# First loads over two queues in another order, later sums of squares, and a later turn of the decay sums in a hybrid attention layer

## The chip, the core and the metric

The kernel runs on one core of a Trainium2 chip. The metric is device time in microseconds (us) for one execution. In the profile, PE is TensorE's matmul and PEld its weight load, ACT is ScalarE, DVE is VectorE, POOL is GpSimd, and SP is SyncE, which here only issues DMAs. A "q" behind an engine's name (ACTq) marks what its queue issues. Each engine works through its own queue in order.

## What is computed

One layer of a streaming encoder on x (512 frames by 1024 channels) and mem (256 memory tokens by 1024 channels), all in float32:

```python
u = rmsnorm(h, g_mix[l])
proj = u @ w_in[l]
(gq, gk, gv, gg, ga, fq, fk, fv, ff, mq, gates) = split_cols(proj, PROJ_SIZES)
...
log_a = jax.nn.log_sigmoid(ga @ w_alpha_up[l] + b_alpha[l]) / GLA_TAU
...
log_f = jax.nn.log_sigmoid(ff + b_forget[l])
o_fox = forgetting_attention(
...
mkv = rmsnorm(mem, g_mem[l]) @ w_mem_kv[l]
mk, mv = jnp.split(mkv, 2, axis=-1)
...
merged = gt[:, :, 0] * y_gla + gt[:, :, 1] * y_fox + gt[:, :, 2] * y_mem
h = h + merged @ w_out[l]
u2 = rmsnorm(h, g_ffn[l])
h = h + jnp.square(jax.nn.relu(u2 @ w_ff1[l])) @ w_ff2[l]
```

Branch A is a gated linear attention ("gla"), branch B the forgetting attention ("fox"), whose logits carry differences of F, the running sum of log_f over the frames; branch C attends to the memory tokens. Only the beginning matters here: the memory's keys and values, u, and the first projections.

## The kernel before

**Products.** Each float32 product is done with three matmuls on a high and a low part (`mm3`, L149 to L152: high x high, high x low, low x high). A weight block is 128 x 1024 float32, 512 KB. It is loaded (`raw`), ACT copies it to its rounded high part (`first_high`, or L141 for later blocks), and DVE subtracts to get the low part (`first_low`, L303, or L142). `gT` (L154) holds weights still and streams activations; `gN` (L164) does the reverse. Both are generators: one *unit* is the three matmuls for one block of 128 input channels, and the caller decides how many units PE gets before the next piece of work. PE's order is the order in which the program is written. PSUM has a pool of four banks with the tag "mm" and one of four with the tag "a".

**The first part** (L348 to L441) stands in `in_order`, which keeps ACT, DVE and PE in the written order. In this order:

- PE runs 12 warm-up matmuls on zeros (L327).
- ACT issues the DMA of `cols` (the gains, 16 KB). w0, the first weight block, is loaded in four quarters, three issued from ACT and the fourth from SP (`first_load(0, 4)`); mem comes from SP in four pairs of channel blocks (256 KB each) into `sg[0]` to `sg[2]` and `dct`. Then SP issues w1, w2, x's first pair, w3, x's other three pairs, the constants `cst`, and w4.
- For each of the 8 channel blocks of mem, ACT makes the high part times its gain (L370) and DVE the low part (L371), with the four quarters of w0 split in between; then w1, w2.
- Four key products of the memory, `mk_proj(0)` to `mk_proj(3)`, 24 matmuls of 256 columns each. Each holds one "mm" bank until `mk_take` (L342) copies it out on ACT. Between them stand the sums of squares of x (`x_squares`: square on ACT at L222 or L225, addition on DVE at L226) and the splits of w3 and w4.
- `rms_cols` (L231) adds up the squares over the partitions with PE; DVE and POOL (a power, L238) make 1/rms per frame. Then come the load and split of w5 and the loads of the rest.
- The memory's values, `mv`: 16 units of three matmuls with 512 columns, four for each of w4 to w7, into two "mm" banks. After six units, `bcast_rows` spreads 1/rms over the partitions (four scaled diagonals on ACT at L246, matmuls at L247, a copy to `rxb` at L249); w6 and w7 are split around it.
- `x_high` (L414 on DVE, L415 on ACT) and `x_low` (L418 on DVE) make u from x for each of 8 blocks; the splits of `both` (the block of the two low-rank projections; L426 on ACT, L428 on DVE), w9 and w10 (the first fox query and key weights) stand between them.

**The second part** (L650 on) runs the low-rank projection (L465, L466) interleaved with the first fox query and key, then fox's values `fv`, 32 units, with other work between them: after 4 units `decay_logs`, after 10 more `decay_sums` (running sums over frames on PE at L495 and L496, then a chain of small additions into `Fc` on DVE, L499 to L504), after 2 more `decay_rows` (PE turns `Fc` at L508, ACT negates it at L509 and issues seven small DMAs at L514). `mem_split` then squares mem on ACT and adds on DVE (L634 to L638), sums on PE (L231 again), and, in its second step, scales the memory's keys and values. `tc.issue_after(i)` makes what is written in its block wait in the queue behind instruction `i` on `i`'s engine, and on that engine alone.

ACT, DVE and POOL are ordered by the compiler's planner in the second part, PE by hand.

Of the kernel before, what the change touches and what calls it, by code (L numbers as in the profile page):

```python
# [61 lines left out]
def hybrid_block(ctx, tc, chunks, wst, xT, memT, xN, cols, gffn, gfin, wup, cst, out):  # L62
    nc = tc.nc
# [213 lines left out]
    with pool("front") as fp:  # L277
        rxb = sg[3]
        xr = fp.tile([P, KT, S], F32, name="xr")
        FIRST_W = [chunks[j] for j in range(8)] + [("G",), ("T", "w_in", OFF["fq"]), ("T", "w_in", OFF["fk"])]  # L280
        raws, ready, loads = {}, {}, {}

        def first_load(i, n=1):
            late = i in (3, 4, 7, 10)
            raws[i] = (fp if late else wp).tile([P, 1024], F32, tag="lead" if late else "raw", name=nm("raw"),
                                                bufs=2 if late else 3)
            for j in range(n):
                sl = slice(j * 1024 // n, (j + 1) * 1024 // n)
                loads[i] = (nc.scalar if n > 1 and j < 3 else nc.sync).dma_start(raws[i][:, sl], wst[index[FIRST_W[i]]][:, sl]).ins
                if n > 1:  # L290
                    yield

        def first_high(i, n=1, j=0):
            if i not in ready:
                ready[i] = [wp.tile([P, 1024], F32R, tag=g, name=nm(g)) for g in ("hi", "lo")]
            sl = slice(j * 1024 // n, (j + 1) * 1024 // n)
            cast = nc.scalar.copy(ready[i][0][:, sl], raws[i][:, sl])
            if i > 4:
                next_sum(cast.ins)

        def first_low(i, n=1, j=0):
            sl = slice(j * 1024 // n, (j + 1) * 1024 // n)
            nc.vector.tensor_tensor(ready[i][1][:, sl], raws[i][:, sl], f(ready[i][0][:, sl]), op=ALU.subtract)  # L303

        def first_split(i, n=1, j=0):
            first_high(i, n, j)
            first_low(i, n, j)

        def first_w(i):
            run(first_load(i))  # L310
            first_split(i)

        get_plain = get_w

        def get_first(key):
            return ready[FIRST_W.index(key)]

        get_w = get_first
        mxh = fp.tile([P, KT, M], F32R, name="mxh")
        mxl = fp.tile([P, KT, M], F32R, name="mxl")  # L320
        xacc = dct[:, :S]
        warm = fp.tile([P, 1], F32, name="warm")
        nc.vector.memset(warm, 0.0)
        wz = fp.tile([P, 512], BF16, name="wz")
        nc.gpsimd.memset(wz, 0.0)
        ps = at_()
        for _ in range(12):  # L327
            nc.tensor.matmul(ps, wz[:, :P], wz, start=True, stop=True)

        kv = {}  # L330

        def mem_in(k):
            return sg[k // 2][:, k % 2 * M:k % 2 * M + M] if k < 6 else dct[:, 4 * S + (k - 6) * M:4 * S + (k - 5) * M]

        def mk_raw(h):
            return gkT[h // 2][:, (h % 2) * M:(h % 2) * M + M]

        def mk_proj(h):
            return gT(("T", "w_mem_kv", P * h), mxh, mxl, lambda ps: kv.update({h: ps}), n=M)

        def mk_take(h):
            nc.scalar.copy(mk_raw(h), kv[h][:, :M])  # L342

        def x_squares(*ks):
            for k in ks:
                sq_col(fp, xr, S, k, xacc, "x")

        with in_order():  # L348
            nc.scalar.activation(warm, warm, AF.Exp)
            nc.scalar.dma_start(cols_s, cols)  # L350
            quarters = first_load(0, 4)
            for j in range(4):
                to = sg[j] if j < 3 else dct[:, 4 * S:5 * S]
                nc.sync.dma_start(to.rearrange("p (k t) -> p k t", k=2), memT[:, 2 * j:2 * j + 2])
                next(quarters)

            def x_load(j):
                nc.sync.dma_start(xr[:, 2 * j:2 * j + 2], xT[:, 2 * j:2 * j + 2])

            run(first_load(1), first_load(2))  # L360
            x_load(0)
            run(first_load(3))
            for j in range(1, 4):
                x_load(j)
            nc.sync.dma_start(cst_s[:, :2 * P], cst[:, :2 * P])
            nc.sync.dma_start(cst_s[:, 5 * P:], cst[:, 5 * P:])
            run(first_load(4))
            for k in range(KT):
                m = mem_in(k)
                nc.scalar.mul(mxh[:, k, :], m, gmem[:, k:k + 1])  # L370
                nc.vector.scalar_tensor_tensor(mxl[:, k, :], m, gmem[:, k:k + 1], f(mxh[:, k, :]),  # L371
                                               op0=ALU.mult, op1=ALU.subtract)
                if k % 2 == 0:
                    first_split(0, 4, k // 2)
            first_split(1, 2, 0)
            first_split(1, 2, 1)
            first_split(2)
            x_squares(0, 1)
            run(mk_proj(0))
            first_split(3)  # L380
            x_squares(2, 3)
            run(mk_proj(1))
            x_squares(4, 5, 6, 7)
            run(mk_proj(2))
            mk_take(0)
            mk_take(1)
            first_split(4)
            run(mk_proj(3))
            rx = rms_cols(fp, xacc, S)
            first_w(5)  # L390
            mk_take(2)
            mk_take(3)
            mv = gN([("N", "w_mem_kv", 2 * j, 512) for j in range(4)], of(mxh, mxl), 2, mmt,
                    lambda t, ps: kv.update({("v", t): ps}))
            for i in (6, 7):
                run(first_load(i))
            g_raw = load_w(("G",))
            for i in (9, 10):
                run(first_load(i))
            run(islice(mv, 6))  # L400
            put = bcast_rows(fp, rx, S, rxb)
            next(put)
            first_high(6)
            first_high(7)
            run(put)
            first_low(6)
            run(islice(mv, 6))
            with tc.issue_after(loads[7]):
                nc.sync.dma_start(cst_s[:, 2 * P:5 * P], cst[:, 2 * P:5 * P])
                nc.sync.dma_start(wup_s, wup)  # L410
            ends = {}

            def x_high(k):
                nc.vector.scalar_tensor_tensor(xr[:, k, :], xr[:, k, :], gmix[:, k:k + 1], rxb, op0=ALU.mult, op1=ALU.mult)  # L414
                ends[0] = nc.scalar.copy(uhi[:, k, :], xr[:, k, :]).ins  # L415

            def x_low(k):
                ends[1] = nc.vector.tensor_tensor(ulo[:, k, :], xr[:, k, :], f(uhi[:, k, :]), op=ALU.subtract).ins  # L418

            x_high(0)  # L420
            x_high(1)
            first_low(7)
            run(mv)
            x_low(0)
            raw3, w3 = (t.rearrange("p (k c) -> p k c", k=KT) for t in (g_raw, both))
            nc.scalar.copy(both, g_raw)  # L426
            low = slice(64, P)
            nc.vector.tensor_tensor(w3[:, :, low], raw3[:, :, low], f(w3[:, :, low]), op=ALU.subtract)  # L428
            first_high(9)
            x_high(2)  # L430
            x_low(1)
            first_low(9)
            x_high(3)
            x_low(2)
            first_split(10)
            for k in range(4, KT):
                x_high(k)
                x_low(k - 1)
            x_low(KT - 1)
            for t in range(2):  # L440
                nc.scalar.copy(gqT[t], kv["v", t])  # L441
        u_ends = ends[0], ends[1]
        get_w = get_plain
# [15 lines left out]
    with pool("fox") as xp:  # L459
# [32 lines left out]
        def decay_sums():  # L492
# [6 lines left out]
            nc.vector.tensor_copy(Fc[:, 0, :], cum[:, 0, :])  # L499
            nc.vector.tensor_copy(off[:, 0, :], tot[:, 0, :])  # L500
            for t in range(1, NT):
                nc.vector.tensor_tensor(Fc[:, t, :], cum[:, t, :], off[:, t - 1, :], op=ALU.add)
                if t < NT - 1:
                    nc.vector.tensor_tensor(off[:, t, :], tot[:, t, :], off[:, t - 1, :], op=ALU.add)  # L504

        def decay_rows():
            psT = at_()
# [121 lines left out]
        def mem_split():  # L629
            own = xp.tile([P, 4, M], F32, tag="nFb", name="memsum", bufs=4)  # L630
            acc, rmb = own[:, 0, :], own[:, 3, :]
            for k in range(KT):
                if k == 0:
                    nc.scalar.activation(acc, mem_in(0), AF.Square)  # L634
                else:
                    sq = own[:, 1 + k % 2, :]
                    nc.scalar.activation(sq, mem_in(k), AF.Square)
                    nc.vector.tensor_tensor(acc, acc, sq, op=ALU.add)  # L638
            rm = rms_cols(xp, acc, M)
            yield  # L640
            run(bcast_rows(xp, rm, M, rmb, 2))
# [11 lines left out]
        with tc.issue_after(u_ends[0]), tc.issue_after(u_ends[1]):  # L653
# [3 lines left out]
            z_end = decay_logs()  # L657
            run(islice(fv, 10))
            nc.vector.tensor_copy(msk_s, cst_s[:, 5 * P:5 * P + 64])
        decay_sums()  # L660
        run(islice(fv, 2))
        decay_rows()
        mem = mem_split()
        with tc.issue_after(z_end[0]), tc.issue_after(z_end[1]):
            next(mem)
        run(fv)
        run(fox_pair(1))
        run(mem)
# [922 lines left out]
```

## Time and profile before

| | |
|---|---|
| time, median of 3 runs | 808.89 us (808.88 to 809.57) |
| the profiled execution | 809.36 us |
| its span | 807.6 us |
| instructions | 12080 |
| busy DVE, ACT, POOL | 574.9, 458.3, 107.2 us |
| DMA traffic | 161.01 MB, mean 199 GB/s |

A row of a timeline has the start in us from the beginning of the span, the duration in us, the engine, the line, the operation, the tiles (written <- read), the shape and a count where several in a row are merged; in square brackets stands the idle time of the engine just before, and what ended it. A row of the waits says who waited for whom, for how long in total, how often, and the longest. A row of the windows has the stretch, its length, then for PE, PEld, DVE, ACT and POOL the busy time and the count of instructions, PE's granted clock, the DMA engines' share and GB/s. Instructions of one engine overlap a little: the next one starts some 0.1 us before the end of the one before.

### The profile page before, as it was taken

The page shows a single profiled execution, that of the slowest core. Times are in us where ns is not written, and L with a number is a line of the kernel's source. Part 1 is how long each engine was busy: PE and PEld are TensorE (multiplying, and loading weights), DVE is VectorE, ACT ScalarE, POOL GpSimd, SP SyncE. Part 2 cuts the span into 40 slices and gives each one's busy share as a digit, 9 for nine tenths or more (in the row PEclk, how much of TensorE's full clock was granted, in tenths as well). Part 3 has the DMA queues.
Part 4 walks back from the last instruction along what each step waited for, and adds up shares of the span by engine and source line. Part 5 has one row for each costly group of instructions (what it writes and reads, how often), then busy time and mean ns, then how long its engine had stood idle before and what let it go on. Part 6 is the DMA issues. An engine that isn't in the chain of part 4 may idle for free.

```text
span 807.6 us, 12080 instructions
## 1 busy us (share of the span) xinstructions
PE 795.8 (99%) x4617; PEld 679.5 (84%) x4617; DVE 574.9 (71%) x877; ACT 458.3 (57%) x727; POOL 107.2 (13%) x124
## 2 busy tenths in 40 slices
PE   9999999999999999999999999999999999999995
PEld 6887878778888888888888889988998899889984
DVE  6763756554565488496969658885788678878886
ACT  7575645533454446454645545764676477547764
POOL 0004221011001132111210000011001100100122
PEclk9999999999999999999999999999999999999998
DMA  9527779678668678889873706889668956895585
GB/s 338 210 92 228 236 228 241 202 209 215 203 209 225 194 218 172 177 212 235 213 179 106 285 3 222 228 197 212 218 176 190 249 196 166 196 258 185 152 153 147
DMA packets 41178, 161.01 MB, mean 199 GB/s; under 512 B 4968, under 2 KB 6048, under 8 KB 39072
## 3 DMA queue, kind: packets, MB, share of 16 engines
q0 software_dynamic: 11632, 60.56, 36.6%
q1 hardware_dynamic: 27504, 95.31, 33.8%
q10 hardware_dynamic: 1984, 4.37, 1.6%
q8 instruction: 36, 0.59, 0.3%
q14 instruction: 22, 0.18, 0.1%
HBM read 156.26 MB, written 31.49 MB: 232 GB/s over the span
## 4 chain that ended last, share of the span: by engine, by line
PE 93%; DVE 2%; DMA 1%; ACT 1%; issue 1%; SPq 0%; POOLq 0%; DVEq 0%; ACTq 0%
PE mm L150 20%; PE mm L151 19%; PE mm L152 19%; PE a L152 4%; PE a L150 4%; PE a L151 4%; PE mm L1020 3%; PE mm L1018 3%; PE mm L1019 3%; PE a L1018 2%; PE a L1020 2%; PE a L1019 2%; PE mm L1391 1%; PE a L616 1%; DMA raw<-in_wst_dram 1%
## 5 line engine op out<-in xcount | busy, mean ns | idle before, releaser
L201 ACT CAST hi<-raw 128x1024 fp32r<-128x1024 f32 x77 | 80.9, 1050 | 62.3 <-PE mm L151 34.3
L202 DVE TENSOR_TENSOR lo<-raw,hi 128x1024 fp32r<-128x1024 f32 x77 | 94.2, 1223 | 29.9 <-ACT hi L201 29.9
L142 DVE TENSOR_TENSOR wlo<-raw,whi 128x1024 fp32r<-128x1024 f32 x44 | 56.7, 1291 | 63.9 <-ACT whi L141 56.8
L141 ACT CAST whi<-raw 128x1024 fp32r<-128x1024 f32 x44 | 46.2, 1050 | 77.0 <-issue 27.5
L152 PE MATMUL mm<-u2h,lo 128*128 128x256 f32 x224 | 63.4, 283 | 0.0
L151 PE MATMUL mm<-u2l,hi 128*128 128x256 f32 x224 | 63.4, 283 | 0.0
L150 PE MATMUL mm<-u2h,hi 128*128 128x256 f32 x224 | 63.4, 283 | 0.0
L1303 POOL DMA_DIRECT2D Y<-in_wst_dram x32 | 27.4, 856 | 262.6 <-DVE lo L202 187.0
L201 ACT CAST hi<-Y 128x1024 fp32r<-128x1024 f32 x34 | 35.6, 1048 | 32.5 <-PE mm L152 22.0
L202 DVE TENSOR_TENSOR lo<-Y,hi 128x1024 fp32r<-128x1024 f32 x34 | 41.6, 1223 | 17.3 <-ACT hi L201 17.3
L150 PE MATMUL mm<-hi,ch 128*128 128x512 f32 x128 | 49.8, 389 | 0.0
L151 PE MATMUL mm<-lo,ch 128*128 128x512 f32 x128 | 49.8, 389 | 0.0
L152 PE MATMUL mm<-hi,cl 128*128 128x512 f32 x128 | 49.8, 389 | 0.0
L201 ACT CAST hi<-g 128x1024 fp32r<-128x1024 f32 x30 | 31.6, 1054 | 30.9 <-PE mm L1020 11.7
L202 DVE TENSOR_TENSOR lo<-g,hi 128x1024 fp32r<-128x1024 f32 x30 | 36.6, 1221 | 17.2 <-ACT hi L201 17.1
L150 PE MATMUL mm<-u2sh,hi 128*128 128x256 f32 x168 | 47.5, 283 | 0.0
L151 PE MATMUL mm<-u2sl,hi 128*128 128x256 f32 x168 | 47.5, 283 | 0.0
L152 PE MATMUL mm<-u2sh,lo 128*128 128x256 f32 x168 | 47.5, 283 | 0.0
L150 PE MATMUL mm<-uhi,whi 128*128 128x512 f32 x112 | 44.4, 397 | 0.0
L152 PE MATMUL mm<-uhi,wlo 128*128 128x512 f32 x112 | 43.7, 390 | 0.0
L151 PE MATMUL mm<-ulo,whi 128*128 128x512 f32 x112 | 43.6, 389 | 0.0
L151 PEld LDWEIGHTS mm<-u2l,hi 128*128 128x128 f32 x224 | 43.0, 192 | 0.2
(446 smaller groups left out, 2329.1 us busy)
## 6 DMA issues: line engine op xcount, KB each, us to landing
raw<-in_wst_dram SPq DMA_DIRECT2D x109, 512.0 KB, 4.9
Y<-in_wst_dram POOLq DMA_DIRECT2D x32, 512.0 KB, 5.4
raw<-T SPq DMA_DIRECT2D x28, 512.0 KB, 3.2
T<-in_wst_dram POOLq DMA_DIRECT2D x12, 1024.0 KB, 8.8
g<-in_wst_dram POOLq DMA_DIRECT2D x24, 512.0 KB, 5.9
Y<-in_wst_dram SPq DMA_DIRECT2D x16, 512.0 KB, 6.3
g<-in_wst_dram SPq DMA_DIRECT2D x12, 512.0 KB, 3.2
nFb<-dF ACTq DMA_DIRECT2D x8, 448.0 KB
```

The source lines that it names most:

```text
L141: cast = nc.scalar.copy(hi, raw)
L142: nc.vector.tensor_tensor(lo, raw, f(hi), op=ALU.subtract)
L150: nc.tensor.matmul(ps, lh, rh, start=start, stop=False)
L151: nc.tensor.matmul(ps, lh, rl, start=False, stop=False)
L152: nc.tensor.matmul(ps, ll, rh, start=False, stop=stop)
L201: nc.scalar.copy(hi, src)
L202: return nc.vector.tensor_tensor(lo, src, f(hi), op=ALU.subtract).ins
L616: nc.tensor.matmul(po[half[e], kt * P:], V[:, kt, 2 * j + e, :], PT[e][:, c0:c0 + S - kt * P], start=kt == 0, stop=kt == 3, skip_group_che ...
L1018: nc.tensor.matmul(ps[t], a, wh[:, kk, :], start=go, stop=False, **w)
L1019: nc.tensor.matmul(ps[t], a, wl[:, kk, :], start=False, stop=False, **w)
L1020: nc.tensor.matmul(ps[t], b, wh[:, kk, :], start=False, stop=k == 3, **w)
L1303: nc.gpsimd.dma_start(to, x, accum_op=ALU.add)
```

## The change

- Ten warm-up matmuls instead of 12.
- `cols` is issued from SP, ahead of mem; the first pair of mem goes in two halves; each quarter of w0 is issued before its pair of mem. w4 is loaded ahead of x's last pair and of the first constants, w5 before the values begin.
- w4 is split after six of x's eight squares instead of after all; three units of the values stand ahead of `rms_cols`, and w5 is split ahead of it. The broadcast follows after 8 units of the values instead of 6; w6 is split ahead of it, w7's low part and the cast of `both` directly behind it.
- `decay_rows` follows four units after `decay_sums` instead of two. The memory's squares are ordered behind the last addition of `decay_sums` (`f_end`) instead of the last of `decay_logs`, and the PE step over them (`rms_cols` in `mem_split`) comes 8 units later.

```diff
-        for _ in range(12):
+        for _ in range(10):
             nc.tensor.matmul(ps, wz[:, :P], wz, start=True, stop=True)
...
-            nc.scalar.dma_start(cols_s, cols)
+            nc.sync.dma_start(cols_s, cols)
             quarters = first_load(0, 4)
             for j in range(4):
                 to = sg[j] if j < 3 else dct[:, 4 * S:5 * S]
-                nc.sync.dma_start(to.rearrange("p (k t) -> p k t", k=2), memT[:, 2 * j:2 * j + 2])
+                to = to.rearrange("p (k t) -> p k t", k=2)
                 next(quarters)
+                if j == 0:
+                    for k in range(2):
+                        nc.sync.dma_start(to[:, k, :], memT[:, k])
+                else:
+                    nc.sync.dma_start(to, memT[:, 2 * j:2 * j + 2])
...
             run(first_load(1), first_load(2))
             x_load(0)
             run(first_load(3))
-            for j in range(1, 4):
-                x_load(j)
+            x_load(1)
+            x_load(2)
+            run(first_load(4))
+            x_load(3)
             nc.sync.dma_start(cst_s[:, :2 * P], cst[:, :2 * P])
             nc.sync.dma_start(cst_s[:, 5 * P:], cst[:, 5 * P:])
-            run(first_load(4))
...
             run(mk_proj(1))
-            x_squares(4, 5, 6, 7)
+            x_squares(4, 5)
+            first_split(4)
+            x_squares(6, 7)
             run(mk_proj(2))
             mk_take(0)
             mk_take(1)
-            first_split(4)
             run(mk_proj(3))
+            run(first_load(5))
+            mv = gN([("N", "w_mem_kv", 2 * j, 512) for j in range(4)], of(mxh, mxl), 2, mmt,
+                    lambda t, ps: kv.update({("v", t): ps}))
+            run(islice(mv, 3))
+            first_split(5)
             rx = rms_cols(fp, xacc, S)
-            first_w(5)
             mk_take(2)
             mk_take(3)
-            mv = gN([("N", "w_mem_kv", 2 * j, 512) for j in range(4)], of(mxh, mxl), 2, mmt,
-                    lambda t, ps: kv.update({("v", t): ps}))
             for i in (6, 7):
                 run(first_load(i))
...
-            run(islice(mv, 6))
+            run(islice(mv, 5))
+            first_split(6)
             put = bcast_rows(fp, rx, S, rxb)
             next(put)
-            first_high(6)
             first_high(7)
             run(put)
-            first_low(6)
+            first_low(7)
+            nc.scalar.copy(both, g_raw)
             run(islice(mv, 6))
...
             x_high(1)
-            first_low(7)
             run(mv)
             x_low(0)
             raw3, w3 = (t.rearrange("p (k c) -> p k c", k=KT) for t in (g_raw, both))
-            nc.scalar.copy(both, g_raw)
...
             for t in range(1, NT):
-                nc.vector.tensor_tensor(Fc[:, t, :], cum[:, t, :], off[:, t - 1, :], op=ALU.add)
+                end = nc.vector.tensor_tensor(Fc[:, t, :], cum[:, t, :], off[:, t - 1, :], op=ALU.add).ins
                 if t < NT - 1:
                     nc.vector.tensor_tensor(off[:, t, :], tot[:, t, :], off[:, t - 1, :], op=ALU.add)
+            return end
...
                     nc.vector.tensor_tensor(acc, acc, sq, op=ALU.add)
+            yield
             rm = rms_cols(xp, acc, M)
             yield
...
-        decay_sums()
-        run(islice(fv, 2))
+        f_end = decay_sums()
+        run(islice(fv, 4))
         decay_rows()
         mem = mem_split()
-        with tc.issue_after(z_end[0]), tc.issue_after(z_end[1]):
+        with tc.issue_after(z_end[0]), tc.issue_after(f_end):
             next(mem)
+        run(islice(fv, 8))
+        next(mem)
         run(fv)
         run(fox_pair(1))
         run(mem)
```

## The prediction

> **What bounds the kernel now.** I read the page first: engine totals, then the list of what PE waited for.
>
> ```profile
> PE 795.8 (99%) x4617; PEld 679.5 (84%) x4617; DVE 574.9 (71%) x877; ACT 458.3 (57%) x727; POOL 107.2 (13%) x124
> ...
> PE a L508 <- DVE Fc L502: 1.3, 1, 1.3
> PE a L328 <- POOL wz L325: 1.3, 1, 1.3
> PE a L231 <- DVE dct L226: 0.7, 1, 0.7
> ```
>
> PE is busy for 99% of the span, and that list of its waits is complete: three waits, all in the first 63 us. So no edit can win more than the late start of the real matmuls and the two waits at L231 and L508, and a wait that the edit creates in the front costs its full length. The change aims at exactly these three places. I take them in order of time, from the timelines of the single engines.
>
> ```profile
> 0.00:20.00 20.00, 18.51 (x108) 13.87 (x108) 12.82 (x24) 15.25 (x29) 0.73 (x5) 1.00 0.92 338
> 6.20:12.40 6.20, 6.20 (x37) 5.00 (x37) 5.87 (x14) 5.92 (x14) 0.00 (x0) 1.00 1.04 405
> ...
> 0.91 0.38 ACTq L350 DMA_DIRECT2D cols_s<-in_cols_dram  x1
> 1.32 5.03 PE L328 MATMUL a<-wz 128*128 128x512 bf16 x12 [1.32 <-POOL wz L325]
> 5.75 0.40 ACT L297 CAST hi<-raw 128x256 fp32r<-128x256 f32 x1 [0.78 <-DMA raw<-in_wst_dram]
> 6.20 0.39 PE L150 MATMUL mm<-mxh,hi 128*128 128x256 f32 x1
> ```
>
> In the windows the last two columns are the DMA share and GB/s: from 6.2 to 12.4 us all 16 DMA engines are full, at 405 GB/s, and the x loads further below, one each 1.3 us, show the same rate to 17.5. In that stretch a load can only come earlier if another comes later.
>
> **First loads and warm-up.** Two warm-up matmuls fewer save 2 x 0.42 us (5.03 us for 12); PE would be free at 5.5 instead of 6.35 us. The issue of cols (0.38 us) leaves ACT's queue, so the first quarter of w0 is issued 0.42 us earlier, and it no longer has cols ahead of it there; cols now stands on SP ahead of mem, at the same 0.4 us. SP issues one DMA more (mem pair 0 in two halves), some 0.4 us, while it has others in flight. The first real matmul waited for this quarter: the cast at 5.75 us ended DMA idle time and the matmul followed at 6.20. So real work begins 0.4 (issue alone) to 0.7 us (PE free) earlier; 0.6 taken. The last pair of mem now goes behind the fourth quarter, and everything after comes out of the full stream, so I let only 0.2 us of this reach the end of the four memory keys (0 to 0.6): PE gets there at 19.6 instead of 20.53 - 0.70 = 19.83. What stands next decides whether that counts.
>
> **x's squares and the turn of order at 20 us.**
>
> ```profile
> 16.14 1.16 ACT L225 ACTIVATE sq<-xr 128x512 f32<-128x512 f32 x2 [0.18 <-DMA xr<-in_xT_dram]
> 17.46 1.29 ACT L225 ACTIVATE sq<-xr 128x512 f32<-128x512 f32 x2 [0.16 <-DMA xr<-in_xT_dram]
> 18.66 0.63 ACT L342 COPY gkT<-mm 128x256 f32<-128x256 f32 x2
> 15.80 4.67 DVE L226 TENSOR_TENSOR dct<-dct,sq 128x512 f32<-128x512 f32 x6
> 20.39 1.22 DVE L303 TENSOR_TENSOR lo<-raw,hi 128x1024 fp32r<-128x1024 f32 x1
> 20.53 1.05 PE L231 MATMUL a<-cst_s,dct 128*128 128x1 f32 x8 [0.70 <-DVE dct L226]
> 21.44 0.48 PE L150 MATMUL mm<-hi,mxh 128*128 128x512 f32 x1
> ```
>
> Before, PE waits 0.70 us for the last sum of squares, runs L231 in 0.91 us, and begins the memory values at 21.44. Now three units of values (3 matmuls of 0.23 us each, 0.69 a unit) stand ahead of L231. They need three things. (a) w4 and its split: w4 is now loaded ahead of x's last pair, so it lands at about 17.46 and that pair one 512 KB place later, 17.46 + 1.32 = 18.78. (b) w4's low part: DVE does it after four of the six sums, 15.80 + 4 x 0.78 = 18.9, done 20.1; the last two sums end at 20.1 + 2 x 0.78 = 21.7 instead of 20.47. (c) a PSUM bank: the pool for these has four, the four key products fill them, and the first comes free with the first L342 copy, which in ACT's order stands behind the squares of x's last pair: 18.78 + 1.16 - 0.09 + 0.35 = 20.2. So (c) is last: the values begin at 20.2, whether PE was ready at 19.2 or 19.8. The 0.70 us wait is replaced by one of about 0.6. The three units end at 20.2 + 2.07 = 22.27, when the sums (21.7) are there, and L231 starts then: 1.74 us later than before, while PE's own work is 21.44 + 2.07 - (22.27 + 0.91) = 0.33 us ahead.
>
> **What hangs on L231.**
>
> ```profile
> 21.86 1.94 POOL L238 TENSOR_TENSOR rr<-ms,cst_s 128x4 f32<-128x4 f32 x1 [20.59 <-DVE ms L237]
> 23.83 1.28 ACT L246 ACTIVATE dg<-cst_s,rr 128x128 f32<-128x128 f32 x4 [1.67 <-POOL rr L238]
> 25.02 1.98 ACT L297 CAST hi<-raw 128x1024 fp32r<-128x1024 f32 x2
> 25.68 1.05 PE L247 MATMUL a<-dg,cst_s 128*128 128x128 f32 x8
> 26.49 0.48 PE L150 MATMUL mm<-hi,mxh 128*128 128x512 f32 x1
> 26.09 1.23 DVE L303 TENSOR_TENSOR lo<-raw,hi 128x1024 fp32r<-128x1024 f32 x1 [3.16 <-ACT hi L297]
> 27.52 1.42 DVE L414 SCALAR_TENSOR_TENSOR xr<-xr,cols_s,sg 128x512 f32<-128x512 f32 x2 [0.21 <-ACT sg L249]
> 28.85 1.22 DVE L303 TENSOR_TENSOR lo<-raw,hi 128x1024 fp32r<-128x1024 f32 x1
> 29.98 0.69 DVE L418 TENSOR_TENSOR ulo<-xr,uhi 128x512 fp32r<-128x512 f32 x1
> 35.97 1.23 DVE L303 TENSOR_TENSOR lo<-raw,hi 128x1024 fp32r<-128x1024 f32 x1 [1.04 <-ACT hi L297]
> 37.27 0.48 PE L152 MATMUL a<-uhi,lo 128*128 128x512 f32 x1
> ```
>
> POOL's power, the four diagonals and the broadcast follow L231; with +1.74 the diagonals run from 25.57 to 26.85. The split of w6 comes ahead of them and costs nothing: ACT had 1.67 us and DVE 3.16 us of idle time just there (were that gone, 1.05 and 1.14 us). PE does five units, 23.18 + 3.45 = 26.6, then L247 (0.81) to 27.45. ACT casts w7 behind the diagonals until 27.85; DVE now takes w7's low part (1.13 us apart) ahead of the first x product instead of after two of them, so that product starts at 28.97 instead of 27.52, and the first ulo 1.43 us later, at 30.4 instead of 29.98: the chain from x to u is 0.42 us late. The cast of "both", now ahead of uhi on ACT, ends at 29.3 and is hidden (uhi is asked at 29.7). DVE then has the same work in a row as before until w10's low part, which ended at 37.20, and PE took it at 37.27, with no slack worth the name. PE arrives 8 units later from 27.45, 0.4 us early, and waits until w10's low part, 37.6: **the front loses 0.4 us** although PE's two waits there got smaller. Its bounds: -0.4 (L231 at 21.4, the sums' earliest) to +0.8.
>
> **The turn of the decay sums.**
>
> ```profile
> 58.96 1.22 DVE L142 TENSOR_TENSOR wlo<-raw,whi 128x1024 fp32r<-128x1024 f32 x1
> 59.88 0.48 PE L150 MATMUL mm<-whi,uhi 128*128 128x512 f32 x1
> 60.09 0.95 DVE L638 TENSOR_TENSOR memsum<-memsum 128x256 f32<-128x256 f32 x2
> 60.96 0.16 DVE L499 COPY Fc<-a 128x8 f32<-128x8 f32 x1
> 61.14 0.42 DVE L638 TENSOR_TENSOR memsum<-memsum 128x256 f32<-128x256 f32 x1
> 62.55 0.16 DVE L502 TENSOR_TENSOR Fc<-a,off 128x8 f32<-128x8 f32 x1
> 62.85 0.27 PE L508 MATMUL a<-cst_s,Fc 128*32 128x128 f32 x1 [1.33 <-DVE Fc L502]
> 63.45 4.08 ACTq L514 DMA_DIRECT2D dF<-dct  x7
> ```
>
> The Fc steps are 0.16 us each but stand between memory's sums (0.42), 0.53 us apart. With those behind f_end the first Fc copy comes at 60.2, after the low part at 58.96, and the last at about 61. PE reaches L508 after four units at 59.88 + 4 x 0.69 = 62.6: **the 1.33 us wait goes**, with 1.6 us to spare. The two added units are work that came later before; they cost nothing. What was hidden is now late: memory's seven adds run from 61 at 0.53 us, to 64.7, and PE asks at L231 (memory's) 8 units after L508, 62.9 + 5.5 = 68.4. Queued behind the new wait on DVE are w's low parts, for PE from 67 us on, and on ACT the squares that wait for buffers. If ACT's seven issues for dF (4.08 us) go in between, memory's sums end at 68.8 and PE waits 0.4 us; I take 0.
>
> **Sum.** -1.33 + 0.4 = -0.9 us. The profiled execution took 809.36 us (span 807.6, 1.8 around it); 0.47 above the median of 808.89, to which I apply the same difference: **808.0 us**. About 0.2% (1.6 us) is what a measurement of this kernel tells from no change: below 807.3 is faster, above 810.5 slower.
>
> **Two rules against this change.** The windows show 338 GB/s in the first 20 us against 405 when full, so the start has room for an earlier stream. The Trainium skill, "DMA: Bandwidth & Descriptors", section "Issuing engines are not separate DMA queues", says that loads from several issuing engines share the same 16 DMA engines, and that a second queue saves only issue time. By it the second case below is worth 0.4 us of issue at the start and nothing at the squares: 808.0; by the rows alone up to 2.1 us in all. The other is on the warm-up: those run 512 columns in 0.42 us, values of that width follow at 0.23. The Trainium skill, "TensorE: Matmul & The Clock Gate", Part 1: The HAM clock gate (the "warmup" mystery), says that PE runs at half rate until a free-running window of about 3.4 us was busy. Here the slow rate lasted through twelve, 5 us; ten make 4.2 us, one window and little more, so a later rise is the fourth case.
>
> **Rivals.**
> - *Forecast, 45%*: 808.0 (807.4 to 808.6): L508's wait goes, the x chain gives 0.4 back.
> - *The front pays as well, 27%*: the early start carries into the stream. For it: the first 20 us moved 338 GB/s against 405 once full, so there is room at the start. Against: the x loads are held by 405 GB/s. If all x loads land 0.6 to 1.2 us earlier, L231 and the chain move by as much: 0.2 to 0.8 gained, total -1.5 to -2.1, 807.4 to 806.8; 807.0 as its time.
> - *x's last pair comes later still, 10%*: it now stands on SP behind w4, whose issue came at 10.96, and SP issues in order.
> ```profile
> 6.79 1.60 SPq L358 DMA_DIRECT2D xr<-in_xT_dram  x3
> 10.96 0.33 SPq L289 DMA_DIRECT2D raw<-in_wst_dram  x1
> ```
>   Before, x's last was issued by 8.4 and w4 2.6 us later. If SP's hold ahead of w4 now comes ahead of x's last load and the stream runs dry, each place of 1.3 us is paid in full through (c). From a first square at 19.8 on, the whole change is slower; two places (21.4) give +1.7, 810.6.
> - *PE's clock rises late, 5%*: if two warm-ups fewer leave the second 24 key products at half rate too, 256 columns in 0.21 instead of 0.115 us, they lose 2.3 us, PE comes to the values at 21.9 instead of 20.2, and the chain is 1.7 later: 809.7.
> - *Memory's sums are late, 10%*: the 0.4 us wait at memory's L231: 808.4.
> - *The turn does nothing, 3%*: Fc stays late behind other DVE work, 809.3.
>
> Faster by over 0.2%: the second case, 0.27; slower: the third, 0.10; the rest, 0.63. The range reaches from the better part of the second case, 806.7, to the last, 809.4; outside it lie the third case, the fourth and the ends.
>
> **What would show it.** PE's list of waits without L508 and L231, and a gap of some 0.6 us at the first matmul of the values near 20.2 us, ended by ACT's copy at L342; ACT's squares of x's last pair near 18.8; the first x product on DVE near 29; PE at w10's low part near 37.6; L508 right behind its unit. A first x product before 28.4 would make the front a gain, one after 30.4 would eat what L508 gives.

## The result and the profile after

The changed kernel took 813.98 us (median of 6 runs, 813.06 to 814.9), the kernel before beside it 809.25 us (6 runs, 808.88 to 810.8): a ratio of 1.0057, 95% interval 1.0044 to 1.0070. It is slower by 4.7 us; 808.0 was forecast. The profiled execution took 813.63 us, its span is 811.9 us against 807.6, so the traces have 4.3 us to account for.

PE's list of waits in the kernel after:

```profile
PE a L231 <- DVE memsum L647: 2.5, 1, 2.5
PE a L328 <- POOL wz L325: 1.3, 1, 1.3
PE mm L150 <- ACT hi L297: 1.0, 2, 0.7
PE a L610 <- DVE P L602: 0.5, 1, 0.5
PE a L152 <- DVE lo L303: 0.5, 1, 0.5
```

The wait for `Fc`, 1.33 us before, is gone as planned. Two others are new in the second part: 2.5 us for the memory's sums at L231, and 0.5 us for `P` at L610. These two less the one that is gone come to 1.7 us. Of the rest, 1.7 us are in no list of waits. PE's timeline:

```profile
63.62 0.27 PE L517 MATMUL a<-cst_s,Fc 128*32 128x128 f32 x1
...
68.97 0.39 PE L152 MATMUL mm<-whi,ulo 128*128 128x512 f32 x1
71.87 0.61 PE L231 MATMUL a<-cst_s,memsum 128*128 128x1 f32 x4 [2.51 <-DVE memsum L647]
```

L517 (L508 of before) has no idle time; L231 has 2.51 us. What follows it is read from the windows, where the third number from the end is PE's granted clock:

```profile
69.79:73.21 3.42, 1.34 (x8) 1.22 (x9) 1.90 (x4) 1.32 (x3) 0.86 (x1) 1.00 0.57 181
73.21:76.62 3.41, 3.41 (x10) 2.64 (x9) 0.00 (x0) 0.94 (x3) 2.93 (x3) 0.50 1.05 303
76.62:80.03 3.41, 3.41 (x17) 2.83 (x16) 1.39 (x2) 3.41 (x8) 0.55 (x2) 1.00 0.79 228
```

The wait empties most of the stretch from 69.79 to 73.21, and for the next 3.41 us PE has half its clock: 10 matmuls where the next window has 17, half of 3.41 or 1.7 us lost. Before, the wait of 1.33 us at L508 cost no clock.

Why the sums are late stands in the queues of ACT and DVE after:

```profile
63.39 0.72 ACT L646 ACTIVATE memsum<-sg 128x256 f32<-128x256 f32 x2
64.01 0.25 ACT L518 ACTIVATE dct<-a 32x128 f32<-32x128 f32 x1
64.29 4.22 ACTq L523 DMA_DIRECT2D dF<-dct  x7
68.56 0.42 ACT L646 ACTIVATE memsum<-sg 128x256 f32<-128x256 f32 x1 [4.30 <-DMA dF<-dct]
...
69.19 1.03 ACT L141 CAST whi<-raw 128x1024 fp32r<-128x1024 f32 x1
70.29 0.42 ACT L646 ACTIVATE memsum<-dct 128x256 f32<-128x256 f32 x1
```

```profile
61.79 0.17 DVE L510 TENSOR_TENSOR Fc<-a,off 128x8 f32<-128x8 f32 x1
...
69.01 0.96 DVE L647 TENSOR_TENSOR memsum<-memsum 128x256 f32<-128x256 f32 x2 [3.40 <-ACT memsum L646]
70.25 1.22 DVE L142 TENSOR_TENSOR wlo<-raw,whi 128x1024 fp32r<-128x1024 f32 x1 [0.28 <-ACT whi L141]
71.39 0.42 DVE L647 TENSOR_TENSOR memsum<-memsum 128x256 f32<-128x256 f32 x1
```

`f_end` is done at 61.96. Two squares fit on ACT before the turn's copy (L518) and its seven DMA issues, which hold ACT's queue for 4.22 us. The next squares come at 68.56. Then a weight's cast on ACT (69.19) and its low part on DVE (70.25) stand ahead of the last square and the last sum, which ends at 71.81. PE had asked at 69.4.

Last, the front, by the points that the prediction named:

```profile
20.61 0.50 PE L150 MATMUL mm<-hi,mxh 128*128 128x512 f32 x1
22.79 0.94 PE L231 MATMUL a<-cst_s,dct 128*128 128x1 f32 x8
...
38.13 0.50 PE L152 MATMUL a<-uhi,lo 128*128 128x512 f32 x1 [0.52 <-DVE lo L303]
```

The values begin at 20.61, where 20.2 was forecast, and without the forecast gap ahead of them. PE gets to w10's low part at 38.13 instead of 37.27, 0.86 us later. So the spans differ by 0.9 (front) - 1.3 (`Fc`) + 2.5 (the sums) + 1.7 (clock) + 0.5 (L610) = 4.3 us.

### The profile page after: what moved, and what is told of

The parts are those of the page before. It is cut to its first block, busy times and chain, and to the rows that moved or that the text cites. A ratio compares the mean times of both kernels' runs of the same rounds, so it can differ in the third digit from the quotient of the medians.

```text
span 811.9 us, 12077 instructions
## 1 busy us (share of the span) xinstructions
PE 797.6 (98%) x4615; PEld 681.3 (84%) x4615; DVE 577.5 (71%) x877; ACT 458.0 (56%) x727; POOL 104.0 (13%) x124
## 4 chain that ended last, share of the span: by engine, by line
PE 92%; DVE 4%; ACT 1%; issue 1%; DMA 1%; ACTq 0%; POOL 0%; SPq 0%; POOLq 0%; DVEq 0%
PE mm L150 19%; PE mm L151 19%; PE mm L152 19%; PE a L152 4%; PE a L150 4%; PE a L151 4%; PE mm L1030 3%; PE mm L1031 3%; PE mm L1032 3%; PE a L1031 2%; PE a L1030 2%; PE a L1032 2%; PE mm L1403 1%; PE a L625 1%; DMA sg<-in_memT_dram 1%
## 5 line engine op out<-in xcount | busy, mean ns | idle before, releaser
L150 PEld LDWEIGHTS mm<-u2h,hi 128*128 128x128 f32 x224 | 43.0, 192 | 0.2
```

The costliest lines, as they stand in the source:

```text
L150: nc.tensor.matmul(ps, lh, rh, start=start, stop=False)
```

## The experiments

Each run's time is a median, with that of the kernel before beside it on the same chip. The ratio and its interval are taken over all the runs and not from the two medians, so the two can differ by up to 0.0007. Unless said otherwise an edit is made in the kernel before.

**The two parts of the change alone.** The second part, from `f_end` on, moves the turn and the memory's sums and nothing else:

```diff
+            return end
...
+            yield
             rm = rms_cols(xp, acc, M)
...
-        decay_sums()
-        run(islice(fv, 2))
+        f_end = decay_sums()
+        run(islice(fv, 4))
         decay_rows()
         mem = mem_split()
-        with tc.issue_after(z_end[0]), tc.issue_after(z_end[1]):
+        with tc.issue_after(z_end[0]), tc.issue_after(f_end):
             next(mem)
+        run(islice(fv, 8))
+        next(mem)
```

> The kernel before with the turn of the decay sums alone (two units further on, memory's squares behind the last addition, memory's sums 8 units later). Theory A (the loss sits here): L508's 1.33 us go, PE waits about 2.5 us at memory's L231, the clock window with that wait holds too little work, and the next 3.4 us run at half rate, 1.7 us lost; together +2.9 us, about 811.9 to 812.2 against 809.0 of before. Theory B (the loss sits in the first loads): L508's wait goes and little comes back, -1.3 to -0.9 us.

813.47 against 809.28 us, ratio 1.0050 (1.0038 to 1.0062). It has nearly the whole loss by itself. PE's longest wait in it, and the windows behind it:

```profile
PE a L231 <- DVE memsum L639: 2.5, 1, 2.5
```

```profile
70.74:74.15 3.41, 2.93 (x9) 2.54 (x10) 0.58 (x3) 0.00 (x0) 1.08 (x1) 0.50 0.87 316
74.15:77.56 3.41, 3.41 (x9) 2.64 (x9) 0.00 (x0) 2.40 (x5) 2.12 (x3) 0.50 1.00 243
```

The wait is the same 2.5 us, and in this execution the half clock lasted two windows.

The other part, all hunks ahead of `f_end` (their diff stands above):

> The kernel before with the first part's edits alone (warm-up, loads, squares behind three units). Theory A: the chain from x to u is 0.9 us late at w10's low part, as in the changed kernel, so +0.9 us, about 809.9; another 0.5 us may come or go with a wait near 102 us. Theory B: +3 to +4.7 us.

810.28 against 809.28 us, ratio 1.0013 (1.0004 to 1.0021): the front loses, by about 1 us; in its trace PE is at w10's low part at 38.22. The two parts add up to 4.2 + 1.0 = 5.2 us; the whole change lost 4.7.

**Is it the wait or the clock?** Eleven matmuls whose result nobody reads stand in the place of the wait, with the second part of the change alone:

```diff
         run(islice(fv, 8))
+        fill = at_()
+        for _ in range(11):
+            nc.tensor.matmul(fill, uhi[:, 0, :P], uhi[:, 0, :], start=True, stop=True)
         next(mem)
```

> As fox_only, with 11 matmuls of 512 columns whose result nobody reads (2.5 us) just ahead of memory's sums on PE, so that PE is busy while it would wait. Theory A: the same wait in total, but the clock stays at full rate: 1.7 us less than fox_only, +1.2 us against before. Rival (half rate costs nothing here, the wait is all): the same time as fox_only.

810.58 against 809.28 us, ratio 1.0019 (1.0010 to 1.0027). The memory's sums come no earlier, and 11 x 0.23 = 2.5 us of PE are spent where 2.5 us were waited, yet it is 2.9 us faster than the same kernel without them. The two profiled executions differ by 4.0 us: two windows at half clock (3.4 us) and a wait of 0.4 us for `P` (L602 there) are gone. PE's waits in it:

```profile
PE a L328 <- POOL wz L325: 1.3, 1, 1.3
PE mm L150 <- ACT hi L297: 0.6, 1, 0.6
PE a L231 <- DVE dct L226: 0.5, 1, 0.5
```

None for the sums, and the granted clock stays at full speed there. The wait's second price is the clock, one or two windows that cost 1.7 us each.

**Would the sums be in time still later?** In the second part alone, PE's step over the sums goes behind all of fox's values:

```diff
-        run(islice(fv, 8))
-        next(mem)
         run(fv)
+        next(mem)
```

> As fox_only, but PE asks for memory's sums after all of fox's values, 14 units behind L508 instead of 8. Theory A: the sums (ready 8 us after L508) are there, no wait, no half rate, and the gain of L508 stays: -1.3 us, about 807.7. Rival: the wait moves on with the step or to the broadcast behind the next projections: no better than fox_only.

810.40 against 809.28 us, ratio 1.0010 (0.9996 to 1.0024), with single runs from 807.58 to 813.38 us. The gain of 1.3 us that the theory expected isn't there; the rival, that the wait moves on, was right for the profiled run (813.28 us). Its longest wait, and POOL's and ACT's timelines:

```profile
PE a L573 <- ACT memsum L249: 2.3, 1, 2.3
```

```profile
79.97 1.29 POOL L551 TENSOR_TENSOR nFb<-nFb,cst_s 128x512 f32<-128x512 f32 x1 [3.04 <-DMA nFb<-dF]
81.23 0.72 POOL L238 TENSOR_TENSOR rr<-ms,cst_s 128x2 f32<-128x2 f32 x1
```

```profile
81.98 0.69 ACT L246 ACTIVATE dg<-cst_s,rr 128x128 f32<-128x128 f32 x2 [7.45 <-POOL rr L238]
```

The power for the memory (L238) stands in POOL's queue behind an addition for fox that waits for a DMA, so ACT and then PE wait. Here too the clock dropped behind the wait, from 87.77 to 94.59 us. The mean granted clock was 0.997 in the runs of 807.58 and 807.75 us and 0.994 in those of 813.28 and 813.38; which of them had the wait is known for the profiled one alone.

**Only the turn, two units later.** The memory's squares stay behind `decay_logs`:

```diff
-        run(islice(fv, 2))
+        run(islice(fv, 4))
         decay_rows()
```

> The kernel before with one edit: decay_rows four units behind decay_sums instead of two; memory's squares and sums stay where they were. Theory A (the turn itself is good, memory's sums put behind it are what costs): PE asks for Fc at 62.65 us, Fc is there at 62.7, memory's sums at 62.6, so L508's 1.33 us go and nothing comes in their place: -1.3 us, about 807.9. Rival (the two later units only move the wait to another place): 0.

**807.83 against 809.22 us, ratio 0.9982 (0.9973 to 0.9991)**: faster than the kernel before and the kernel after, by 1.4 us against before, where the wait was 1.33. PE's list in full:

```profile
PE a L328 <- POOL wz L325: 1.3, 1, 1.3
PE a L231 <- DVE dct L226: 0.5, 1, 0.5
```

**The squares between the DMA issues.** The second part with the first step of `mem_split` written ahead of `decay_rows`, so that ACT has the squares before or between the seven issues:

```diff
         f_end = decay_sums()
-        run(islice(fv, 4))
-        decay_rows()
         mem = mem_split()
         with tc.issue_after(z_end[0]), tc.issue_after(f_end):
             next(mem)
+        run(islice(fv, 4))
+        decay_rows()
         run(islice(fv, 8))
         next(mem)
```

> As fox_only, but with the first step of mem_split written ahead of decay_rows, so that on ACT memory's squares stand between the seven issues for dF instead of behind them. Theory A (the issues on ACT's queue, 4.3 us, and the weight split behind them make memory's sums late): the sums are ready before PE asks, no wait at memory's L231, no half rate: -1.2 us against before, 5 us less than fox_only. Rival (the order behind f_end alone is too late): a wait of over 1 us stays.

807.77 against 809.22 us, ratio 0.9983 (0.9974 to 0.9992). ACT's timeline in it:

```profile
63.80 0.84 ACTq L515 DMA_DIRECT2D dF<-dct  x2
64.69 0.42 ACT L638 ACTIVATE memsum<-sg 128x256 f32<-128x256 f32 x1 [0.92 <-DVE memsum L639]
64.71 1.81 ACTq L515 DMA_DIRECT2D dF<-dct  x1
...
66.91 0.42 ACT L638 ACTIVATE memsum<-dct 128x256 f32<-128x256 f32 x1
66.92 1.09 ACTq L515 DMA_DIRECT2D dF<-dct  x3
```

The same squares and the same issues, the last square at 66.91 instead of 70.29, and no wait for the sums. So it was the place behind the seven issues that made them late, not the wait for `f_end`. The time is that of the turn alone (807.83): ordering the memory's squares behind `f_end` gains nothing of its own.

The same swap in the changed kernel:

> The changed kernel, with the first step of mem_split written ahead of decay_rows as in fox_swap, all else as changed. Theory A (two independent parts): the second part gives its 1.4 us (fox_swap), the first part costs its 1.0 us (front_only): -0.4 us against before, about 808.8, 5 us less than the changed kernel, and no half rate behind 60 us. Rival (the late first part takes the second part's slack): memory's sums are waited for again, +1 us or more.

809.09 against 809.21 us, ratio 0.9998 (0.9989 to 1.0007): 4.9 us less than the changed kernel measured beside its own before. The front's loss and the turn's gain then about cancel. In its trace PE is at w10's low part at 38.77. PE's waits:

```profile
PE a L328 <- POOL wz L325: 1.3, 1, 1.3
PE a L152 <- DVE lo L303: 0.5, 1, 0.5
PE mm L150 <- ACT gkT L342: 0.5, 1, 0.5
```

**The front in two.** Its start alone: ten warm-up matmuls, `cols` on SP, and the new order of w0 and mem.

> The kernel before with ten warm-ups and the new order of cols, mem's pairs and w0's quarters alone. Theory A (these loads delay the stream of all later ones by 0.4 us, since small rows go first): x's squares and the chain to w10's low part 0.4 us later, +0.4 us. Rival (the earlier first matmul carries through): -0.5 us.

809.76 against 809.22 us, ratio 1.0010 (1.0001 to 1.0018). The first real matmul comes at 5.20 us instead of 6.20, but x's first square at 13.66 instead of 12.24. A window at half clock, 10.25 to 13.66, also falls in this trace, so its later points mix two causes.

The rest of the front alone (w4 ahead of x's last pair, three units ahead of L231, the moved splits), under the old start:

> The kernel before with the rest of the first part alone: w4 loaded ahead of x's last pair, three units of the values ahead of L231, the splits moved. Theory A (x's last pair comes one load later and holds the values through ACT's copy of the first key product; the chain to w10's low part gets later by it): L231 at 22.3, the first x product at 29.0, +0.4 us. Rival (the hidden 0.7 us wait pays): -0.4 us or better.

809.49 against 809.22 us, ratio 1.0005 (0.9996 to 1.0014). PE's and DVE's timelines:

```profile
20.10 0.50 PE L150 MATMUL mm<-hi,mxh 128*128 128x512 f32 x1 [0.25 <-ACT gkT L342]
22.29 0.95 PE L231 MATMUL a<-cst_s,dct 128*128 128x1 f32 x8
```

```profile
28.87 1.41 DVE L419 SCALAR_TENSOR_TENSOR xr<-xr,cols_s,sg 128x512 f32<-128x512 f32 x2
```

Forecast for the whole front were 20.2, 22.27 and 28.97, and 37.6 for w10's low part, which is 37.57 here. So the chain was worked out rightly, for a start that left the stream of loads where it was. This start doesn't.

**What in the start delays the loads?** First the start with mem's first pair as one DMA:

```diff
-                if j == 0:
-                    for k in range(2):
-                        nc.sync.dma_start(to[:, k, :], memT[:, k])
-                else:
-                    nc.sync.dma_start(to, memT[:, 2 * j:2 * j + 2])
+                nc.sync.dma_start(to, memT[:, 2 * j:2 * j + 2])
```

> As front_start, but mem's first pair as one DMA again. If the rows of 1 KB of its halves delay the stream: the bytes moved by 8 us are back at those of before (1840 to 1905 KB against 1523 to 1674 with the new start), +0.2 us or less against before. If the order over the two queues (cols and w0's quarters early, SP's last quarter and pair behind) delays it: they stay near 1600 to 1700 KB, and +0.5 us stays.

809.57 against 809.21 us, ratio 1.0001 (0.9992 to 1.0009); x's first square at 12.62 us. By 8 us it had moved 1.70 MB, where the seven traces with the old start have 1.84 to 1.90 and the four with the new start 1.52 to 1.67. So the two signs that were set beforehand disagree: by its bytes the order over the two queues is at fault, by its time, which is back at that of before, the split of mem's pair. Then the later turn with only the warm-ups and `cols` of the new start:

```diff
-        for _ in range(12):
+        for _ in range(10):
...
-            nc.scalar.dma_start(cols_s, cols)
+            nc.sync.dma_start(cols_s, cols)
...
-        run(islice(fv, 2))
+        run(islice(fv, 4))
         decay_rows()
```

> turn_only with ten warm-ups and cols issued from SP ahead of mem; mem's pairs and w0's quarters in the order of before. If moving cols alone is harmless: w0's first quarter 0.4 us earlier or more, the same bytes by 8 us, the time of turn_only (807.8) within 0.3. If cols in front of mem delays the stream: bytes by 8 us down by 100 KB or more, +0.4 us against turn_only.

808.67 against 809.21 us, ratio 0.9986 (0.9977 to 0.9994), less than the turn alone gives; x's first square at 12.96, in the kernel with the turn alone at 12.29. By 8 us it had moved 1.77 MB, 0.07 to 0.14 less than with the old start, so the limit of 100 KB set beforehand decides nothing. The windows from 6 to 8 us (the last number is GB/s) of the kernel before, the kernel after, and the one with the turn and `cols`:

```profile
6.00:8.00 2.00, 2.00 (x11) 1.31 (x10) 1.82 (x5) 2.00 (x7) 0.00 (x0) 1.00 1.09 407
```

```profile
6.00:8.00 2.00, 1.29 (x7) 0.76 (x6) 1.05 (x3) 1.07 (x4) 0.00 (x0) 1.00 1.07 314
```

```profile
6.00:8.00 2.00, 2.00 (x10) 1.64 (x10) 1.93 (x5) 1.39 (x4) 0.00 (x0) 1.00 1.05 364
```

The old start moves 407 GB/s there (401 to 409 in seven traces), the new one 314 in the kernel after and 300 alone (271 to 314 in four traces), 334 with the pair unsplit, 364 with `cols` and the warm-ups alone. That puts the loss on no single edit. What makes the DMA engines slower there (the sizes of the pieces, the order over the two queues, or what lies in flight at the time) stays open. The rate is clear of the spread between traces, but what comes of it is less so: x's first square lies between 12.12 and 12.61 in the seven traces with the old start, at 12.64 in the kernel after and from 13.30 to 13.66 in the other three with the new one. The ratios of the turn alone and of the turn with `cols` have intervals that overlap.

## Why the prediction was wrong, point by point

- **The wait at L508 goes, -1.33 us: right.** It is in no list of a kernel with the later turn, and the turn alone gives -1.4 us.
- **Memory's sums, taken at 0: this is the step that failed.** The prediction saw the mechanism: ACT's seven issues in between, sums at 68.8, PE asking at 68.4. It chose the case without them, "seven adds run from 61 at 0.53 us, to 64.7", gave the other 10% and priced it at 0.4 us. The case came in full and measured 2.5 us of waiting (asked 69.4, sums 71.81). The size was off because the squares and sums met more work than was counted: behind the issues a weight's cast on ACT, 1.03 us, and its low part on DVE, 1.22 us, stood ahead of the last sum, and ahead of the issues another weight's cast (62.44 us) and low part (63.52). The swap of order settles the cause: with the same DMAs and the squares between them there is no wait, and the changed kernel takes 4.9 us less.
- **The clock behind a long wait: missing.** A late clock was a rival at the start only, 5%. Behind the sums a window at half rate cost 1.7 us more, in one trace two windows; filling the wait won 2.9 us. So the price of the sums, taken at 0, was 4.2 us in the trace of the change. The Trainium skill, "TensorE: Matmul & The Clock Gate", section "HAM oscillation — how this bites in real kernels", gives as its rule no idle gaps of PE over some 3.4 us. By it a wait of 2.5 us would have kept the clock; here it did not, and the measurement decides.
- **The front loses 0.4 us: the mechanism right, the size too small.** It lost 0.86 us in the trace of the whole change, and 1.0 us in the runs of the first part alone. The term that was off is the landing of x's last pair: forecast with the loads' old times plus one place, 18.78, while the squares came at 19.14, as the row below shows; L231 and w10's low part are 0.52 and 0.53 us behind their forecast. Under the old start the same row reads 18.63 and the chain comes out as forecast. How much the new start adds differs from trace to trace (PE is at w10's low part at 38.13, 38.22 and 38.77 in the three kernels with the whole new front, at 37.23 to 37.68 in six with the old one); why it adds it stays open.
```profile
19.14 1.16 ACT L225 ACTIVATE sq<-xr 128x512 f32<-128x512 f32 x2 [0.27 <-DMA xr<-in_xT_dram]
```
- **The rival in which the front pays as well, 27%: wrong.** An earlier first matmul (5.69 instead of 6.20) does not carry into the stream; the loads came later, not earlier. The "room at the start" in the bandwidth was no reserve that this order could use. By the Trainium skill, "DMA: Bandwidth & Descriptors", section "Issuing engines are not separate DMA queues", a second queue saves only issue time. The runs add that another start of the loads over the two queues moved less, 271 to 314 GB/s from 6 to 8 us instead of 401 to 409.
- **x's last pair later still, 10%: not by that mechanism.** SP issued w4 at 8.22 us and x's last pair at 8.78 and did not hold them. The squares of that pair began 0.36 us behind the forecast here, 1.0 us in the first part alone (19.78) and in the changed kernel with the swap (19.81), close to the 19.8 from which on the prediction called the change slower. But from x's first square to them it is 6.5 us in all three, and 6.5 under the old start with the rest of the front: the whole stream was late from the start, and the pair lost no place beyond the one that was forecast.
- **PE's clock rises late, 5%: not in that form.** From 4.94 to 8.36 us the granted clock was 1.00. One window behind it was at half rate:
```profile
8.36:11.77 3.41, 3.41 (x16) 3.27 (x16) 3.41 (x10) 3.41 (x9) 0.00 (x0) 0.50 1.02 414
```
  So the memory's keys ended only at 20.6 us, and PE had no gap ahead of the values. ACT's first copy, which frees the bank, began at 20.20, so little or nothing was lost by it; the trace of the first part alone has no window at half rate, and its loss is as large.
- **The wait at L610, 0.5 us: foreseen by no one.** DVE's and POOL's timelines of the kernel after:
```profile
98.39 1.35 DVE L602 TENSOR_SCALAR P<-P,ri 128x128 f32<-128x128 f32 x2
...
99.73 2.87 DVE L602 TENSOR_SCALAR P<-P,ri 128x256 f32<-128x256 f32 x5
```
```profile
98.09 1.30 POOL L559 TENSOR_TENSOR nFb<-nFb,cst_s 128x512 f32<-128x512 f32 x1 [7.00 <-DVE ri L601]
100.29 1.30 POOL L559 TENSOR_TENSOR nFb<-nFb,cst_s 128x512 f32<-128x512 f32 x1 [0.90 <-DMA nFb<-dF]
```
  and of the kernel before, where POOL's addition begins only at 96.51, in the last 0.4 us of that stretch:
```profile
94.60 0.54 DVE L593 TENSOR_SCALAR P<-P,ri 128x128 f32<-128x128 f32 x2
...
95.12 1.80 DVE L593 TENSOR_SCALAR P<-P,ri 128x256 f32<-128x256 f32 x5
```
  The same scaling takes 1.35 + 2.87 instead of 0.54 + 1.80 us, 1.9 us more, where two additions of POOL lie beside it; PE needs the result. The delay of what came before had put the two side by side; the second part alone has the wait too (0.4 us, the same scaling 1.52 + 2.75 us beside POOL's additions at 99.00 and 100.51), the kernels with the turn alone and with the swapped order have none there. It was not tried by itself.

## What to carry to other kernels

When work is ordered behind a later instruction on an engine, write down the whole queue that then stands ahead of its last piece, DMA issues and other casts included, and price the case that this queue is met in full, not the case that it is missed. A wait on PE of over two us may cost its length and then 1.7 us for each of one or two windows at half clock, so the worst place for it is a stretch with no other slack. When a change has several parts, look at each alone: here one line (the turn two units later) was worth -1.4 us, and the rest cost 6.1 us, over four times as much.

## What the runs showed of the hardware that was not expected

- **The clock is granted in steps of 3.41 us, and less than a whole empty window is enough to lose it.** In the window 69.79 to 73.21 of the kernel after, PE began four matmuls of 512 columns (72.33 to 73.11), which at 0.22 us each fill about a quarter of it (the row's busy time, 1.34 us, also counts their overlapping ends and L231), and the next window ran at half rate. The stretches at half rate in these traces are 3.41 us long or twice that (70.74 to 77.56 with the second part alone, 87.77 to 94.59 with PE's step behind all values). Counted in columns, windows of 25 to 31% were followed by half the clock in the kernel after (also 4.94 to 8.36, behind which the memory's keys ran at half rate), with the second part alone, and with the new start alone. Before, the window with the 1.33 us wait was filled to 39%, and the clock stayed; four other traces with windows of 38 or 39% kept it too:

```profile
60.56:63.97 3.41, 2.08 (x13) 1.50 (x12) 2.56 (x13) 2.44 (x5) 0.69 (x2) 1.00 0.61 226
```

  One window that was followed by a half one (84.35 to 87.77 with PE's step behind all values) was filled to 45%, with many matmuls of 64 rows, so the share of columns is not the whole rule. The windows lie differently in each run against the same work, so a wait of this length may or may not meet one; that fits the spread of 5.8 us with PE's step behind all values, but wasn't shown run by run.
- **Seven small DMA issues hold ACT's queue for 4.22 us**, and single ones up to 1.8 us. ACT computes nothing in that time unless the work is written between them.
- **An addition on POOL stretches DVE's scaling beside it**, by 1.9 us for two additions of 1.30 each. The Trainium skill, "SBUF — State Buffer", section "SBUF: two separate sides", says that VectorE in some of its operations and GpSimd share a pair of ports, which one holds for a whole instruction while the other blocks. The trace agrees: the piece of the scaling that began beside each addition ended only behind it (98.39 + 1.08 us, the addition at 99.39; 100.31 + 1.50 us, the addition at 101.59). That this scaling is one of those operations no run here shows.
